# Where a streaming attention step turns its cached keys: TensorE or VectorE

## The chip, the cores and the metric

The kernel runs on one core of a Trainium2 chip. A core has five engines that run side by side, each with its own queue of instructions: TensorE (PE in the profile, with its weight loads as a row of their own, PEld), VectorE (DVE), ScalarE (ACT), GpSimd (POOL) and SyncE (SP), which here issues most of the transfers. The metric is the device time of one execution in microseconds, as the median of several runs.

## The reference, cut to what matters

One layer takes 512 new frames of one stream (the prompt) and 64 next frames of another (the samples), which has 512 cached frames. Both go through the same weights. The attention part, for each of 8 heads of 128 channels, is a stick-breaking attention:

```
z = jnp.einsum('bqhd,bkhd->bhqk', q, k) / math.sqrt(HEAD_DIM)
mask = (k_pos[None, :] < q_pos[:, None])[None, None]
log_1mb = jnp.where(mask, jax.nn.log_sigmoid(-z), 0.0)
after = lax.cumsum(log_1mb, axis=3, reverse=True) - log_1mb
w = jnp.where(mask, jnp.exp(jax.nn.log_sigmoid(z) + after), 0.0)
return jnp.einsum('bhqk,bkhd->bqhd', w.astype(v.dtype), v)
```

The samples' queries see the 512 cached keys and the 64 new ones. Beside it stands a gated convolution over 1024 channels; the outputs of both are normed, put side by side and multiplied by one output projection, and a SwiGLU feed-forward layer follows:

```
mix = jnp.concatenate([rmsnorm(o_attn, g_attn_out), rmsnorm(o_conv, g_conv_out)], axis=-1)
x = x + mix @ w_out
h2 = rmsnorm(x, g_norm2)
x = x + (jax.nn.silu(h2 @ w_gate) * (h2 @ w_up)) @ w_down
```

All data is fp32.

## The kernel before, in words

Prompt and samples lie side by side, channels on the 128 partitions and 576 frames along the free axis (512 prompt, 64 samples). A large product takes each fp32 operand as two fp32r parts, a high one (`whi`, `qh`, `ph`), cast by ACT, and a low one (`wlo`, `ql`, `pl`), the difference, taken by VectorE; three products of parts make one. That pairing of a cast and a subtraction is the helper `split`, and its two lines (L228, L229) appear under most of the names below.

The stages follow one another: the input projection (to about 570 us of the span), the convolution's half of the output projection (`out_proj(mixed_conv, ...)`, to about 748 us), the attention's half, then the feed-forward layer. The attention itself has no stage of its own. It runs inside the convolution's half of the output projection, woven between that half's products.

How it is woven: TensorE's instructions stay in the order in which the program writes them. `product` issues three matmuls of 128x288 and then ticks a counter (`pipe.tick()`); this is a *step*. Generators are registered with the counter; each `yield n` hands back control until n steps later. `heads()` starts one `attend(h)` every 29 steps (`PERIOD`), and one head's generator lasts longer than that, so the end of a head runs among the start of the next. The instructions of ACT, VectorE, GpSimd and SP are not held to the written order: a scheduler places them when the program is built, by its own estimate of when each will be ready. `tc.issue_after(x)` tells it to place what follows behind instruction x. Once placed, an engine runs its queue in order, and a waiting instruction holds all behind it.

One head, in its steps:

- Scores of the prompt, in three blocks (`scores`, L1176 and L1173), each followed by `softplus`: three ACT steps (L1131 to L1133) and one on VectorE (L1134) that reads `z` and writes `pr`. Block 2 comes first.
- Seven steps after its start the samples' scores, `zs` (L1204): one product of the new keys `kf` and four of the cached keys `kcT`, each fp32 and so of two passes, ten passes in all. Then the next head's `qf` and `kf` are loaded into the same buffers.
- The cached keys arrive in `cK` with frames on the partitions (four blocks of 128 frames by 128 channels). The products need channels on the partitions. `keys_cached` has TensorE turn the four blocks into a PSUM buffer `kc` of the pool `ps_pj` (three buffers, shared with the projection's `pjo` and the head's `po`), and ACT copies it to `kcT` (L1157, L1158). Head h does this for head h + 1, and then loads head h + 2's `cK`.
- Sums along the stick (`trir`, `neg1r`), a mask by VectorE (L1229), the exponential (L1231) and a `split`, for each block.
- The prompt's output `po` (L1283) in three parts, with `sample_weights` in between: the samples' sums, a mask on VectorE (L1223) and one exponential on ACT that writes `ws` (L1225).
- `mixed(po, ...)` scales the output into the high and low parts `mixa` (L1273, L1274); squares follow for the norm.
- Two steps later, the samples' output `os_` (L1298): four products of the cached values `cV` and one of the new ones `vtok`, ten passes, each with a part of `ws`. Then `fetch_v` loads the next head's values into the same buffers.

The samples' output of a head and the samples' scores of the next head fall on the same step, 36 steps after the start of the first and 7 after that of the second.

Of the kernel before, what the change touches and what calls it, by code (L numbers as in the profile page):

```python
# [22 lines left out]
BK = 32  # L23
D = 2048
KD = D // P
NH = 8
# [76 lines left out]
def tile_hybrid_stream_step(  # L103
# [6 lines left out]
    nc = tc.nc  # L110
# [3 lines left out]
    ck, cv = cache_k[0, 0], cache_v[0, 0]  # L114
# [26 lines left out]
    def misc(name):  # L141
        return ps_z.tile([P, 512], F32, tag="misc", name=name, bufs=2)
# [84 lines left out]
    def split(hi, lo, src, lo_eng=None):  # L227
        cast = nc.scalar.copy(out=hi, in_=src)  # L228
        (lo_eng or nc.vector).tensor_tensor(out=lo, in0=src, in1=hi.bitcast(F32), op=ALU.subtract)  # L229
        return cast.ins  # L230
# [6 lines left out]
    ident = const.tile([P, P], F32, name="ident")  # L237
# [395 lines left out]
    with tc.manual_schedule(engines={mybir.EngineType.Activation, mybir.EngineType.DVE, mybir.EngineType.SP}):  # L633
# [60 lines left out]
        for kt in range(KD + LAG):  # L694
# [22 lines left out]
            if kt in (7, 11, 17):  # L717
                j = (kt - 7) // 4
# [300 lines left out]
    cK = bpool.tile([P, 4, P], F32, name="cK")  # L1019
    ws = bpool.tile([P, 320], F32, name="ws")  # L1020
    kcT = bpool.tile([P, TP], F32, name="kcT")
    neg1r, trir = (bpool.tile([P, P], F32R, name=name) for name in ("neg1r", "trir"))
    m01, mneg = (bpool.tile([P, P], F32, name=name) for name in ("m01", "mneg"))
    s01, sneg = (bpool.tile([P, TS], F32, name=name) for name in ("s01", "sneg"))
# [14 lines left out]
        split(kh, kl, kf[:, :TP])  # L1039

    def load_cached_keys(h):
        nc.sync.dma_start(out=cK, in_=ck[:, h, :].rearrange("(i p) d -> p i d", p=P))

    def fetch_v(h):
        first = nc.sync.dma_start(out=vtok[:, 4], in_=v_dram[h][T - P :])
# [36 lines left out]
    for h in range(NH):  # L1082
        t = tpool.tile([P, 2, T], F32R, tag=f"t{h}", name=f"mixa{h}")
# [46 lines left out]
    def softplus(dst, ps, scratch):  # L1130
        nc.scalar.activation(out=scratch, in_=ps, func=AF.Abs)  # L1131
        nc.scalar.activation(out=scratch, in_=scratch, func=AF.Exp, scale=-1.0)
        nc.scalar.activation(out=scratch, in_=scratch, func=AF.Ln, bias=1.0)  # L1133
        nc.vector.scalar_tensor_tensor(out=dst, in0=ps, scalar=0.0, in1=scratch, op0=ALU.max, op1=ALU.add)  # L1134

    kw = dict(start=False, skip_group_check=True)
    bt = {}
# [13 lines left out]
        split(bt["v2"][:, 0], bt["v2"][:, 1], vtok[:, 0:2, :])  # L1151
        split(bt["vh"][2], bt["vl"][2], vtok[:, 2, :])

    def keys_cached(h):
        kc = ps_pj.tile([P, 512], F32, tag="pj", name="kc")
        for i in range(4):
            nc.tensor.transpose(kc[:, i * P : (i + 1) * P], cK[:, i, :], ident)  # L1157
        nc.scalar.copy(out=kcT, in_=kc)  # L1158
        if h + 1 < NH:
            load_cached_keys(h + 1)  # L1160

    width = (512, 384, 256)
    full = (512, 384, 384)
# [1 line left out]
    def attend(h):  # L1165
        pr, ph, pl, s1h, s1l, sp = (bt[n] for n in ("pr", "ph", "pl", "s1h", "s1l", "sp"))
        pb = [pr[0], pr[1], pr[2][:, :256], pr[2][:, 256:]]
        z, zb = {}, {}

        def scores(i):  # L1170
            kk, q0 = slice(i * P, (i + 1) * P), i * P
            if i == 3:
                mm(zb[i], kf[:, kk], qf[:, q0:TP], stop=False, **kw)  # L1173
                return
            for n, (a_, b_) in enumerate(((kh, qh), (kh, ql), (kl, qh))):
                mm(zb[i], a_[:, kk], b_[:, q0:TP], start=(n == 0), stop=False, skip_group_check=True)  # L1176

        for b in (2, 1, 0):
            z[b] = ps_z.tile([P, 512], F32, tag=f"z{b}", name=f"z{b}")
            zb[b] = z[b][:, : width[b]]  # L1180
            if b == 2:
                zb[3] = z[b][:, 256:384]
            blocks = (2, 3) if b == 2 else (b,)
            w = full[b]
            for i in blocks:
                scores(i)
            softplus(pr[b][:, :w], z[b][:, :w], pr[b][:, :w])
            for i in blocks:
                nc.gpsimd.tensor_tensor(out=pb[i][:, :P], in0=pb[i][:, :P], in1=m01, op=ALU.mult)  # L1189
            split(ph[b], pl[b], pr[b][:, : width[b]])  # L1190
            if b == 2:
                nc.gpsimd.tensor_tensor(out=pb[2][:, P:], in0=pb[2][:, P:], in1=pb[3], op=ALU.add)
                split(s1h, s1l, pb[2])
            if b == 1:
                nc.gpsimd.tensor_tensor(out=pb[1][:, P:], in0=pb[1][:, P:], in1=pb[2], op=ALU.add)
                split(s0h, s0l, pb[1])
            yield 3 if b else 1
            if h == 0 and b == 1:
                keys_cached(0)

        zs = misc("zs")
        for n, b in enumerate((4, 3, 2, 1, 0)):
# [15 lines left out]
        def sample_weights():  # L1218
            mm(zs[:, :320], trir, sph[:, :320], stop=False, **kw)
            mm(zs[:, :320], trir, spl[:, :320], stop=False, **kw)  # L1220
            mm(zs[:, :256], neg1r, sph[:, 320:], stop=False, **kw)
            mm(zs[:, :256], neg1r, spl[:, 320:], stop=True, **kw)
            nc.vector.scalar_tensor_tensor(out=zs[:, 256:320], in0=zs[:, 256:320], scalar=0.0, in1=sneg,  # L1223
                                           op0=ALU.min, op1=ALU.add)
            nc.scalar.activation(out=ws, in_=zs[:, :320], func=AF.Exp)  # L1225
# [12 lines left out]
        mm(zb[3], trif, pb[3], stop=False, **kw)  # L1238
        mm(zb[2][:, P:], neg1f, pb[3], stop=False, **kw)
# [2 lines left out]
        behind = weights(2)  # L1242
# [8 lines left out]
        behind = weights(1)  # L1251
# [27 lines left out]
        po = ps_pj.tile([P, 512], F32, tag="pj", name="po")  # L1279
        mm(po[:, 384:512], vtok[:, 3, :], pb[3], start=True, stop=False, skip_group_check=True)  # L1280
        for i in (2, 1, 0):
            for n, (a_, b_) in enumerate(((vh, ph), (vl, ph), (vh, pl))):
                mm(po[:, i * P : 512], a_[i], b_[i][:, : 512 - i * P], stop=(i == 0 and n == 2), **kw)  # L1283
# [12 lines left out]
        for b in range(5):  # L1296
            lv = vtok[:, 4, :] if b == 4 else cV[:, b, :]
# [442 lines left out]
```

## Time and profile before

| | us |
|---|---|
| median of 3 runs | 2326.66 (2326.58 to 2326.91) |
| the profiled execution | 2327.18 |
| its span, first to last instruction | 2325.5 |
| TensorE busy | 2315.3 |
| TensorE's weight loads busy | 2306.9 |
| VectorE busy | 1951.5 |
| ScalarE busy | 1222.1 |
| GpSimd busy | 304.3 |

The granted TensorE clock is full over the whole span. The difference between the execution's own time and its span, 1.7 us, lies around the first and the last instruction. Matmuls are pipelined, so two in a row overlap in the records: the distance between two starts, and not the duration of one, tells what an instruction takes from TensorE's time.

### The profile page before, as it was taken

Reading aid. Unit: us, or ns where it says so; the run is one execution under the profiler, and the core shown is the slowest. Engines: PE = TensorE matmul, PEld = TensorE weight load, DVE = VectorE, ACT = ScalarE, POOL = GpSimd, SP = SyncE. Lnnn points to the kernel's source line nnn. Section 1 sums busy time; section 2 is a strip of 40 time slices with the busy share of each in tenths; the row PEclk is TensorE's granted clock in tenths of the full one; section 3 lists DMA queues with packets and bytes.
Section 4 is the critical chain, followed back from the end, with each engine's and each line's share of the span. In section 5 each row is a group of like instructions: output and inputs, shape, how many; then the busy total and the mean of one; then the engine's idle time right before and its main releaser. Section 6 shows DMA issues by size and latency. Waiting matters only on the chain.

```text
span 2325.5 us, 43556 instructions
## 1 busy us (share of the span) xinstructions
PE 2315.3 (100%) x17432; PEld 2306.9 (99%) x17432; DVE 1951.5 (84%) x2871; ACT 1222.1 (53%) x2170; POOL 304.3 (13%) x374
## 2 busy tenths in 40 slices
PE   9999999999999999999999999999999999999999
PEld 9999999999999999999999999999999999999999
DVE  8898989897777898888888888888888777987897
ACT  8566656456887564444444444444444444444443
POOL 0212121110432320000000000000000002431222
PEclk9999999999999999999999999999999999999999
DMA  8444343546653554544444444344344936885654
GB/s 273 136 118 130 91 142 107 147 129 209 191 148 101 173 200 128 155 138 141 149 135 150 131 148 155 112 157 157 117 155 134 351 129 205 228 240 184 209 128 108
DMA packets 533674, 368.57 MB, mean 158 GB/s; under 512 B 70246, under 2 KB 517888, under 8 KB 533472
## 3 DMA queue, kind: packets, MB, share of 16 engines
q1 hardware_dynamic: 526976, 356.42, 48.8%
q0 software_dynamic: 6384, 9.24, 2.3%
q8 instruction: 136, 2.23, 0.4%
q14 instruction: 66, 0.54, 0.1%
q10 hardware_dynamic: 112, 0.14, 0.0%
HBM read 285.52 MB, written 80.23 MB: 157 GB/s over the span
## 4 chain that ended last, share of the span: by engine, by line
PE 94%; ACT 3%; DVE 2%; POOL 1%; issue 0%; DMA 0%; SPq 0%; POOLq 0%; ACTq 0%; DVEq 0%
PE psy L405 47%; PE psw L405 24%; PE psx L405 12%; PE pjo L224 6%; PE pj L691 1%; PE pjz L691 1%; PE psv L405 1%; PE pjm L691 1%; ACT ph L228 0%; PE psx L556 0%; DVE pr L1134 0%; DVE wlo L177 0%; POOL pr L1189 0%; ACT whi L176 0%; DMA vtok<-v_dram 0%
## 5 line engine op out<-in xcount | busy, mean ns | idle before, releaser
L229 DVE TENSOR_TENSOR whl<-raw_a,whl 128x1024 fp32r<-128x1024 f32 (+4 forms) x384 | 429.8, 1120 | 55.5 <-ACT whl L228 54.1
L405 PE MATMUL psy<-t,whl 128*128 128x288 f32 x3000 | 447.0, 294 | 0.0
L228 ACT CAST whl<-raw_a 128x1024 fp32r<-128x1024 f32 (+4 forms) x384 | 360.1, 940 | 140.0 <-PE psx L405 44.9
L405 PE MATMUL psy<-h_s,whl 128*128 128x288 f32 x2766 | 416.6, 294 | 0.0
L405 PEld LDWEIGHTS psy<-t,whl 128*128 128x128 f32 x3000 | 414.4, 188 | 0.0
L405 PE MATMUL psw<-t,whl 128*128 128x288 f32 x2688 | 388.9, 294 | 0.0
L405 PEld LDWEIGHTS psy<-h_s,whl 128*128 128x128 f32 x2766 | 383.1, 188 | 0.2
L405 PEld LDWEIGHTS psw<-t,whl 128*128 128x128 f32 x2688 | 366.8, 188 | 0.0
L228 ACT CAST whl<-raw_b 128x1024 fp32r<-128x1024 f32 (+5 forms) x234 | 211.4, 905 | 208.2 <-issue 71.4
L229 DVE TENSOR_TENSOR whl<-raw_b,whl 128x1024 fp32r<-128x1024 f32 (+5 forms) x234 | 256.1, 1095 | 73.4 <-ACT whl L228 72.4
L428 ACT COPY part<-psy 128x288 f32<-128x288 f32 x309 | 123.2, 399 | 347.9 <-PE psy L405 345.5
L405 PE MATMUL psx<-h_s,whl 128*128 128x288 f32 x1164 | 170.2, 294 | 0.0
L228 ACT CAST whl<-s 128x1024 fp32r<-128x1024 f32 (+5 forms) x103 | 95.3, 925 | 124.3 <-PE psw L405 116.4
L405 PEld LDWEIGHTS psx<-h_s,whl 128*128 128x128 f32 x1164 | 159.6, 188 | 0.0
L405 PE MATMUL psw<-t34a,whl 128*128 128x288 f32 x1056 | 150.4, 295 | 0.0
L405 PE MATMUL psy<-t12a,whl 128*128 128x288 f32 x1056 | 150.4, 295 | 0.0
L405 PEld LDWEIGHTS psw<-t34a,whl 128*128 128x128 f32 x1056 | 143.5, 188 | 0.0
L405 PEld LDWEIGHTS psy<-t12a,whl 128*128 128x128 f32 x1056 | 143.3, 188 | 0.2
L1455 POOL DMA_DIRECT2D hid_dram<-form x7 | 5.2, 736 | 951.6 <-DVE form L229 944.5
L229 DVE TENSOR_TENSOR whl<-s,whl 128x1024 fp32r<-128x1024 f32 (+5 forms) x103 | 110.3, 1071 | 20.3 <-ACT whl L228 19.6
L224 PE MATMUL pjo<-mixc,whi 128*128 128x288 f32 x512 | 118.7, 299 | 0.0
L224 PE MATMUL pjo<-mixa,whi 128*128 128x288 f32 x512 | 102.8, 295 | 0.0
(565 smaller groups left out, 3922.0 us busy)
## 6 DMA issues: line engine op xcount, KB each, us to landing
hid_dram<-form SPq DMA_DIRECT2D x147, 288.0 KB
raw_a<-in_w_in_dram SPq DMA_DIRECT2D x22, 1024.0 KB
raw_b<-in_w_in_dram SPq DMA_DIRECT2D x22, 1024.0 KB
raw_b<-in_w_gate_dram SPq DMA_DIRECT2D x22, 1024.0 KB
raw_b<-in_w_up_dram SPq DMA_DIRECT2D x22, 1024.0 KB
raw_a<-in_w_gate_dram SPq DMA_DIRECT2D x22, 1024.0 KB
raw_a<-in_w_up_dram SPq DMA_DIRECT2D x22, 1024.0 KB
h_s<-hid_dram SPq DMA_DIRECT2D x10, 2016.0 KB
```

Source lines behind the costliest of these rows:

```text
L224: mm(ps, w_[:, k, csl], x_[:, a:b], start=(k == 0 and n == 0), stop=(k == nk - 1 and n == 2))
L228: cast = nc.scalar.copy(out=hi, in_=src)
L229: (lo_eng or nc.vector).tensor_tensor(out=lo, in0=src, in1=hi.bitcast(F32), op=ALU.subtract)
L405: mm(ps, whl[:, w_, j, :], x_, start=(start and j == 0 and q == 0), stop=(j == len(xs_) - 1 and q == 2), skip_group_check=True)
L428: nc.scalar.copy(out=t, in_=st["y"])
L691: mm(banks_[c][i], w3[:, kt % 8, c * P : (c + 1) * P], t[:, x_, :], start=(kt == 0 and n == 0), stop=(kt == KD - 1 and n == 2))
L1455: q.dma_start(out=hid_dram[fp][2 * n - 2 : 2 * n].rearrange("f p t -> p f t"), in_=t.bitcast(F32))
```

## The change

The cached keys of head 0 are loaded and turned as before. For heads 1 to 7 the load is in four pieces, each of 32 channels: piece g writes partitions g to g + 31, and on partition j of it stand, for every 32nd frame from j on, 32 channels in a row (runs of 128 bytes). So each block of 32x32 holds what the turned keys need there, only turned within the block, and one stream transpose by VectorE from `cK` to `kcT`, which turns each 32x32 block by itself, does the rest. It is placed behind the head's own softplus of block 2, instead of a step of the head before. The four TensorE transposes, the buffer `kc` and ACT's copy remain in head 0 only.

The samples' output comes three steps after `mixed`, not two. And `mixed(po, ...)` has to be placed behind the samples' mask and exponential.

```diff
@@ load_cached_keys
-        nc.sync.dma_start(out=cK, in_=ck[:, h, :].rearrange("(i p) d -> p i d", p=P))
+        if h == 0:
+            nc.sync.dma_start(out=cK.rearrange("p (i d) -> p i d", d=P), in_=ck[:, h, :].rearrange("(i p) d -> p i d", p=P))
+            return
+        for g in range(0, P, BK):
+            nc.sync.dma_start(out=cK[g : g + BK].rearrange("j (t d) -> j t d", d=BK),
+                              in_=ck[:, h, g : g + BK].rearrange("(t j) d -> j t d", j=BK))
@@ keys_cached, now first_keys
-    def keys_cached(h):
+    def first_keys():
         kc = ps_pj.tile([P, 512], F32, tag="pj", name="kc")
         for i in range(4):
-            nc.tensor.transpose(kc[:, i * P : (i + 1) * P], cK[:, i, :], ident)
+            nc.tensor.transpose(kc[:, i * P : (i + 1) * P], cK[:, i * P : (i + 1) * P], ident)
         nc.scalar.copy(out=kcT, in_=kc)
-        if h + 1 < NH:
-            load_cached_keys(h + 1)
@@ attend
-            softplus(pr[b][:, :w], z[b][:, :w], pr[b][:, :w])
+            behind = softplus(pr[b][:, :w], z[b][:, :w], pr[b][:, :w])
+            if h and b == 2:
+                with tc.issue_after(behind):
+                    nc.vector.transpose(out=kcT, in_=cK)
...
         if h + 1 < NH:
-            keys_cached(h + 1)
+            load_cached_keys(h + 1)
...
-                sample_weights()
+                mask, exp = sample_weights()
                 yield 2
-        mixed(po, 0, TP)
+        with tc.issue_after(mask), tc.issue_after(exp):
+            mixed(po, 0, TP)
         nc.scalar.activation(out=sq[0], in_=po[:, :HALF], func=AF.Square)
         squares(0)
         nc.scalar.activation(out=sq[1][:, : TP - HALF], in_=po[:, HALF:], func=AF.Square)
-        yield 2
+        yield 3
```

How the queues of the built programs differ, at three places (lines of the changed program carry its own numbers). On TensorE, at the step that head 0's output and head 1's scores share, before and then with the change; `pjo` is the projection's product:

```order
L224 MATMUL pjo<-mixc,whi_6605 128x288
L1298 MATMUL zs<-ws,cV 128x64 x4
L1298 MATMUL zs<-ws,vtok 128x64
L1204 MATMUL zs<-qf,kf 128x64
L1204 MATMUL zs<-qf,kcT 128x64 x4
L224 MATMUL pjo<-mixc,whi_6605 128x288
L224 MATMUL pjo<-mixc,wlo_6606 128x288
```

```order
L224 MATMUL pjo<-mixc,whi_6605 128x288
L1210 MATMUL zs<-qf,kf 128x64
L1210 MATMUL zs<-qf,kcT 128x64 x4
L224 MATMUL pjo<-mixc,whi_6605 128x288
L224 MATMUL pjo<-mixc,wlo_6606 128x288
L224 MATMUL pjo<-mixc,whi_6605 128x288
L1305 MATMUL zs<-ws,cV 128x64 x4
L1305 MATMUL zs<-ws,vtok 128x64
```

The scores now stand ahead, and the output behind them and one step of three products; it is so in heads 1 to 7.

On VectorE, at the softplus of block 2 of head 6, with the split of a projection weight (`wlo`) ahead of it:

```order
L177 TENSOR_TENSOR wlo_8233<-raw_a,whi_8232 128x512 x3
L229 TENSOR_TENSOR pl_6703<-pr_6700,ph_6702 128x512
L177 TENSOR_TENSOR wlo_8233<-raw_a,whi_8232 128x512
L1134 SCALAR_TENSOR_TENSOR pr_6701<-z_8251,pr_6701 128x384
L1223 SCALAR_TENSOR_TENSOR zs<-zs,sneg 128x64
L229 TENSOR_TENSOR hbe<-pr_6701,hbe 128x256
```

```order
L177 TENSOR_TENSOR wlo_8219<-raw_a,whi_8218 128x512 x3
L229 TENSOR_TENSOR pl_6703<-pr_6700,ph_6702 128x512
L1139 SCALAR_TENSOR_TENSOR pr_6701<-z_8237,pr_6701 128x384
L1193 STREAM_TRANSPOSE kcT<-cK 128x512
L1229 SCALAR_TENSOR_TENSOR zs<-zs,sneg 128x64
L1115 TENSOR_TENSOR pjo<-pjo,accc 128x288
```

The transpose stands between the softplus and the samples' mask of the head before, in all seven heads; one of the four splits moved away ahead of this piece.

On ACT, at the same place; `ph` is the high part of head 5's block 0, and the L1131 of `z_8251` the first softplus step of head 6:

```order
L1231 ACTIVATE pr_6700<-z_8075 128x512
L176 CAST whi_8232<-raw_a 128x512
L228 CAST ph_6702<-pr_6700 128x512
L1131 ACTIVATE pr_6701<-z_8251 128x384
L1132 ACTIVATE pr_6701<-pr_6701 128x384
```

```order
L1237 ACTIVATE pr_6700<-z_8064 128x512
L1136 ACTIVATE pr_6701<-z_8237 128x384
L228 CAST ph_6702<-pr_6700 128x512
L1137 ACTIVATE pr_6701<-pr_6701 128x384
L1138 ACTIVATE pr_6701<-pr_6701 128x384
```

The two have changed places, and the cast of a weight is gone from between. On ACT the exponential of `ws` stands ahead of `mixa<-po` in both programs. On SP the pieces of a head's cached keys are issued partly ahead of the next head's `qf` and `kf` and partly behind its values; the loads of `vtok` and `cV`, which stood ahead of `qf` and `kf`, now stand behind them.

More of the change, by code (lines that the diff above doesn't have):

```diff
@@ L1018, in tile_hybrid_stream_step @@
     qh, ql, kh, kl = (bpool.tile([P, TP], F32R, name=name) for name in ("qh", "ql", "kh", "kl"))
-    cK = bpool.tile([P, 4, P], F32, name="cK")
+    cK = bpool.tile([P, TP], F32, name="cK")
     ws = bpool.tile([P, 320], F32, name="ws")
@@ L1133, in softplus @@
         nc.scalar.activation(out=scratch, in_=scratch, func=AF.Ln, bias=1.0)
-        nc.vector.scalar_tensor_tensor(out=dst, in0=ps, scalar=0.0, in1=scratch, op0=ALU.max, op1=ALU.add)
+        return nc.vector.scalar_tensor_tensor(out=dst, in0=ps, scalar=0.0, in1=scratch, op0=ALU.max, op1=ALU.add).ins
     kw = dict(start=False, skip_group_check=True)
@@ L1198, in attend @@
             if h == 0 and b == 1:
-                keys_cached(0)
+                first_keys()
         zs = misc("zs")
@@ L1222, in sample_weights @@
             mm(zs[:, :256], neg1r, spl[:, 320:], stop=True, **kw)
-            nc.vector.scalar_tensor_tensor(out=zs[:, 256:320], in0=zs[:, 256:320], scalar=0.0, in1=sneg,
-                                           op0=ALU.min, op1=ALU.add)
-            nc.scalar.activation(out=ws, in_=zs[:, :320], func=AF.Exp)
+            mask = nc.vector.scalar_tensor_tensor(out=zs[:, 256:320], in0=zs[:, 256:320], scalar=0.0, in1=sneg,
+                                                  op0=ALU.min, op1=ALU.add)
+            return mask.ins, nc.scalar.activation(out=ws, in_=zs[:, :320], func=AF.Exp).ins
         def weights(b):
```

## The prediction, made before the changed kernel ran

> **What bounds the kernel now.** I read the page's busy shares first, then the waits of TensorE over the stretch in which the changed functions run, and then that stretch cut at one repeating mark. From the page:
>
> ```profile
> span 2325.5 us, 43556 instructions
> PE 2315.3 (100%) x17432; PEld 2306.9 (99%) x17432; DVE 1951.5 (84%) x2871; ACT 1222.1 (53%) x2170; POOL 304.3 (13%) x374
> ```
>
> TensorE is busy for 2315.3 of 2325.5 us. So time is saved only by taking work off TensorE or by closing gaps in its queue, and lost only by opening gaps. The heads run from about 574 to 750 us. In the list of waits of TensorE's weight loads from 560 to 780 us, all the gaps are small:
>
> ```profile
> PEld zs L1298 <- ACT ws L1225: 2.2, 5, 0.9
> PEld po L1283 <- DVE pl L229: 0.7, 2, 0.4
> PEld po L1283 <- ACT ph L228: 0.5, 1, 0.5
> PEld zs L1204 <- ACT kcT L1158: 0.4, 1, 0.4
> PEld z L1176 <- DVE kl L229: 0.2, 1, 0.2
> ```
>
> Columns: microseconds in total, times, longest. The largest is the samples' output product, L1298, waiting for the samples' weights `ws`. These are waits of the loads, so what they cost has to be read from the pace. I cut the stretch at the first L1298 of heads 0 to 6; each row is one head's period.
>
> ```profile
> 604.89:625.35 20.46, 20.46 (x154) 20.11 (x153) 14.79 (x32) 17.41 (x40) 7.98 (x15) 1.00 0.55 151
> 625.35:646.72 21.37, 21.28 (x154) 20.14 (x152) 15.40 (x32) 17.18 (x40) 8.62 (x15) 1.00 0.53 146
> 646.72:667.32 20.60, 20.60 (x151) 20.07 (x151) 14.96 (x33) 17.02 (x40) 7.94 (x15) 1.00 0.45 110
> 667.32:689.00 21.68, 21.18 (x152) 20.02 (x151) 16.85 (x37) 17.50 (x40) 6.72 (x14) 1.00 0.36 114
> 689.00:710.30 21.30, 20.67 (x152) 20.09 (x152) 16.00 (x36) 17.12 (x39) 6.47 (x14) 1.00 0.39 122
> 710.30:731.20 20.90, 20.72 (x151) 20.13 (x151) 16.84 (x37) 17.14 (x40) 6.86 (x13) 1.00 0.29 96
> ```
>
> Columns: the stretch, its length, then busy time of PE, PEld, DVE, ACT and POOL, granted clock (full), share of the DMA engines, GB/s. The same tensor work is done in each, so the first, 20.46, is a head without a gap, and the others are longer by 0.91, 0.14, 1.22, 0.84 and 0.44: 3.55 us in all is lost to waits. ACT (17 of 20.5) and DVE (15 to 17) are the engines that are waited for.
>
> **The turning taken off TensorE: a gain of 3.05 us.** One group of four transposes, from TensorE's timeline:
>
> ```profile
> 716.09 0.29 PE L224 MATMUL pjo<-mixc,whi 128*128 128x288 f32 x1
> 716.23 0.60 PE L1157 MATMUL kc<-ident,cK 128*128 128x128 f32 x4
> 716.58 0.38 PE L224 MATMUL pjo<-mixc,whi 128*128 128x288 f32 x1
> 716.80 0.29 PE L224 MATMUL pjo<-mixc,wlo 128*128 128x288 f32 x1
> 716.93 0.29 PE L224 MATMUL pjo<-mixc,whi 128*128 128x288 f32 x1
> ```
>
> Durations overlap, so I count starts. The last two starts lie 0.13 apart. From the first `whi` to `wlo` 0.71 us pass where two steps of 0.13 to 0.14 would stand: the group costs 0.44, including the slow first load behind it. Head 0 keeps its group, so 7 x 0.435 = 3.05. [...] With the groups go seven copies of ACT:
>
> ```profile
> L1158 ACT COPY kcT<-kc x8: 566/584/591, 585.2 to 717.8; 128x512 f32<-128x512 f32 x8
> ```
>
> That is 0.58 us less on ACT per head, worth nothing by itself since TensorE is the bound, but it gives room to the engine that is waited for. The PSUM buffer `kc` no longer takes a turn among the three of its pool; no wait for that pool stands above, so nothing is counted.
>
> **The turning put on VectorE: 0.70 us per head, off the path.** A stream transpose on this chip took:
>
> ```profile
> L1608 DVE STREAM_TRANSPOSE ob<-acc_z x2: 465/468/470, 2221.8 to 2227.0; 128x288 f32<-128x288 f32 x2
> L807 DVE STREAM_TRANSPOSE tok<-E-20_1697 x1: 770/770/770, 159.5 to 159.5; 128x576 f32<-128x576 f32 x1
> ```
>
> A column costs (770 - 468) / 288 = 1.05 ns, so 512 columns cost 468 + 224 x 1.05 = 703 ns. It stands right behind the softplus of block 2 (L1134) and ahead of the samples' mask (L1223). Two queues hang on it. First TensorE's sample scores, which read `kcT`. Second, on DVE itself, the mask and all behind it. The tightest head:
>
> ```profile
> 707.96 0.56 DVE L1134 SCALAR_TENSOR_TENSOR pr<-z,pr 128x384 f32<-128x384 f32 x1 [0.21 <-ACT pr L1133]
> 708.43 0.22 DVE L1223 SCALAR_TENSOR_TENSOR zs<-zs,sneg 128x64 f32<-128x64 f32 x1
> ...
> 709.25 0.19 PEld L224 LDWEIGHTS pjo<-mixc,whi 128*128 128x128 f32 x1
> 710.30 0.97 PEld L1298 LDWEIGHTS zs<-ws,cV 128*128 128x128 f32 x8 [0.86 <-ACT ws L1225]
> ```
>
> The transpose would start where the mask does, at 708.43, and end at 709.13. The scores now come first in TensorE's queue, right behind the load at 709.25: 0.14 later, and 0.22 more for the two passes on the new keys, so `kcT` is needed at 709.6. That leaves 0.5 us in the head that waits longest for ACT. So I take nothing lost. Bounds: 0 below, 7 x 0.70 = 4.9 above, if every transpose lay wholly on the path. DVE's load rises to 15.5 to 17.6 of 20, still under ACT's.
>
> **The samples' outputs one step later: a gain of about 2 us.** L1298 moves behind the scores (ten passes) and one step of three products. How long ten passes take:
>
> ```profile
> 747.75 0.29 PE L224 MATMUL pjo<-mixc,whi 128*128 128x288 f32 x1
> ...
> 749.12 0.30 PE L224 MATMUL pjo<-mixa,wlo 128*128 128x288 f32 x1
> ```
>
> Between these lie ten passes and two steps of 0.13: 1.37 - 0.27 = 1.10. So L1298 gets 1.10 + 0.40 = 1.50 us more for `ws`. The longest wait was 0.86 by its row, or 710.30 - 709.25 - 0.14 = 0.91 by starts, and the mask lies at most 0.70 later behind the transpose: 0.91 + 0.70 is 0.1 over the 1.50 in the worst head and under it in all others. I take the whole 2.2 of the list as gone (by starts it is nearer 2.4). Today the twenty passes stand together; in a gapless head, by the same count:
>
> ```profile
> 625.34 0.29 PE L224 MATMUL pjo<-mixc,whi 128*128 128x288 f32 x1
> ...
> 627.84 0.29 PE L224 MATMUL pjo<-mixc,wlo 128*128 128x288 f32 x1
> ```
>
> 2.50 - 0.27 = 2.23 against twice 1.10: parting them costs nothing.
>
> Of the other gaps (`pl`, `ph`, `kl`, 1.3 us together), ACT's and DVE's new order takes some and gives some: the masks of `z` and ACT's exponentials of block 1 come earlier, but block 0's cast `ph` now stands behind the next head's first softplus step, 0.5 us later. One row of DVE against one of TensorE shows what is left at the tightest place:
>
> ```profile
> 706.46 0.69 DVE L229 TENSOR_TENSOR pl<-pr,ph 128x512 fp32r<-128x512 f32 x1
> ...
> 707.56 0.19 PEld L1283 LDWEIGHTS po<-pl,hbe 128*128 128x128 f32 x1
> ```
>
> 707.15 against 707.56: 0.4 of slack, so about 0.1 of new wait there. Given and taken, I count nothing; bounds are a gain of 1.3 and a loss of 0.7, if each of seven heads had only this slack.
>
> **The mixed output queued behind the exponential: nothing.** ACT's order already has `ws` ahead of `mixa<-po` in every head. The new wait only pins it. Behind the waiting `mixa` stand ACT's casts of the next head, and no row of `mixa<-po` is waited for.
>
> **The new loads: nothing.** One load per head becomes four, of 128-byte runs. SP's queue took 0.4 us to issue one load of the old kind:
>
> ```profile
> 686.83 0.38 SPq L184 DMA_DIRECT2D raw_a<-in_w_out_dram  x1
> ...
> 695.54 0.38 SPq L1042 DMA_DIRECT2D cK<-in_cache_k_dram  x1
> 707.83 0.38 SPq L184 DMA_DIRECT2D raw_a<-in_w_out_dram  x1
> ```
>
> SP stood idle for 12 us between the last two, so three more issues of about 0.4 find room. The price on the DMA engines, from a stretch in which only 128-byte runs were stored:
>
> ```profile
> 2230.00:2235.00 5.00, 5.00 (x40) 5.00 (x39) 4.84 (x6) 2.22 (x4) 1.69 (x2) 1.00 0.27 43
> ```
>
> A share of 0.27 for 43 GB/s means 159 GB/s at full share, so 256 KB cost 1.6 us of a 20 us period in which the share is 0.29 to 0.55. The later pieces of a head are issued behind the values' loads, about 15 us ahead of its transpose. Two pieces of head 6, which wait for head 5's transpose, now stand ahead of the weight load that went out at 686.83; it goes out some 5 us later, behind the values, and its slot is read only in the next weight's turn, 20 us on. With that cover gone the transpose would wait and all of DVE behind it. Bounds: 0, and for each us that a landing is late, that us once per head less the slack of 0.5.
>
> **The sum.** Profiled execution 2327.18 us (its span 2325.5 and 1.7 around it). Less 3.05, less 2.2, the other terms zero: 2321.9. That execution lies 0.5 above the median of 2326.66, so for the median 2321.4, 0.23% less.
>
> **Rivals.** *The gaps stay.* Periods of 21 us could be ACT's own pace: 17 busy and in-order waits around it. Then TensorE, 0.44 sooner per head, only waits elsewhere. For it speak the rows of 21.68 and 21.30, where `ph` and `pl` waits join those for `ws`; against it the 20.46 with the same 17.4 on ACT, and that ACT loses 0.58 per head. It gives 2326.66 - 3.05 = 2323.6, and with 0.2 of new waits per head 2325.0.
>
> *VectorE becomes the bound.* The transpose finds DVE late, so sample scores wait for `kcT` in seven heads. Slower by over 0.2% (4.65 us) needs 4.65 + 5.25 = 9.9 us of waits, 1.4 per head: behind a slack of 0.5 or more that means a `kcT` some 2 us late, three DVE instructions of 0.7. For it: three splits of a weight (`wlo`) stand just ahead of that softplus in the tightest head. Against it: there DVE still had an idle 0.21 before L1134. It decides where TensorE's wait for `kcT` exceeds 0.75 per head; at 1.5 per head the time is 2332. [...]
>
> *All gaps close.* ACT's 0.58 of room and the earlier masks also end the waits for `pl`, `ph` and `kl`: 2326.66 - 3.05 - 3.55 = 2320.1. The rows of 20.46 and 20.60 show that gapless heads exist; that `ph` comes 0.5 later speaks against it.
>
> *The queueing does nothing.* The third part's wait pins what is so already, as said; its time is that of the forecast.
>
> **Numbers.** Forecast (a gain of 4 to 6): 0.52. All gaps close: 0.12. Gaps stay: 0.26. VectorE late: 0.10, of which 0.07 beyond +0.2%. The bound of 0.2% is about what a measurement of this kernel can tell from no change. The forecast lies just beyond it, so 0.09 of its own chance counts as same: faster 0.43 + 0.12 = 0.55, same 0.09 + 0.26 + 0.03 = 0.38, slower 0.07. The range goes from 2319.9 (all gaps closed, and 0.2 of head 0's) to 2325.2 (gaps stay, 0.2 per head of new waits); what it leaves out is the late VectorE and a little on each side.
>
> **What would show it.** Right: no L1157 from head 1 on; seven stream transposes of about 0.70 us; no wait of L1298 for `ws`; periods near 20.0. Wrong: TensorE waiting for `kcT` or for `pl` and `ph` in several heads (gaps moved), DVE waiting for a load of `cK` (cover gone), or periods still at 21.

## The result, and the profile after

The changed kernel takes 2322.43 us (median of 16 runs, 2321.55 to 2323.51); the kernel before, run beside it, 2327.81 (16 runs, 2326.58 to 2329.01). The ratio is 0.9977, with a 95% interval from 0.997 to 0.9984: faster by 5.4 us, between 3.7 and 7.0. The profiled execution took 2323.28. From its page:

```profile
span 2321.6 us, 43509 instructions
PE 2310.5 (100%) x17404; PEld 2303.5 (99%) x17404; DVE 1952.7 (84%) x2878; ACT 1216.2 (52%) x2163; POOL 303.7 (13%) x374
```

28 TensorE transposes fewer, 7 VectorE instructions more, 7 ScalarE instructions fewer. The lines of the changed program have other numbers: the samples' scores stand at L1210, their output at L1305, the exponential that writes `ws` at L1231. The waits of TensorE's weight loads, 560 to 780 us, as before (us in total, times, longest):

```profile
PEld zs L1210 <- ACT kcT L1163: 1.0, 1, 1.0
PEld z L1179 <- DVE kl L229: 0.8, 2, 0.4
PEld po L1289 <- DVE pl L229: 0.6, 1, 0.6
PEld po L1289 <- DVE hbe L229: 0.4, 1, 0.4
PEld z L1179 <- ACT kh L228: 0.2, 1, 0.2
```

In this list no product waits for `ws` any more, and none in heads 1 to 7 for turned keys; the wait for `kcT` is head 0's, which TensorE still turns. The new instruction, by its line:

```profile
L1193 DVE STREAM_TRANSPOSE kcT<-cK x7: 700/702/702, 604.4 to 726.5; 128x512 f32<-128x512 f32 x7
```

The stretch cut at the first sample output of heads 0 to 6, as before (length, busy PE, PEld, DVE, ACT, POOL, granted clock, DMA share, GB/s):

```profile
607.69:627.69 20.00, 20.00 (x150) 19.64 (x149) 15.20 (x34) 16.54 (x38) 7.76 (x14) 1.00 0.76 188
627.69:648.56 20.87, 20.52 (x150) 19.76 (x149) 15.58 (x33) 16.63 (x39) 8.23 (x15) 1.00 0.58 145
648.56:668.54 19.98, 19.98 (x150) 19.63 (x148) 16.12 (x35) 16.51 (x39) 8.32 (x14) 1.00 0.66 159
668.54:688.49 19.95, 19.95 (x149) 19.60 (x148) 16.83 (x37) 16.41 (x38) 7.00 (x13) 1.00 0.28 74
688.49:708.85 20.36, 20.22 (x150) 19.52 (x149) 16.80 (x37) 16.31 (x39) 6.49 (x14) 1.00 0.51 154
708.85:728.86 20.01, 20.01 (x150) 19.66 (x149) 16.34 (x36) 15.94 (x37) 5.95 (x12) 1.00 0.33 88
```

A head without a gap now takes 20.0 us, not 20.46. The six periods add up to 121.17 against 126.31: 5.14 less, of which 6 x 0.46 = 2.8 is a gapless head's gain and the remaining 2.4 are gaps that closed. Two gaps are left: 0.87 in the second row (waits for `hbe` and `kl`) and 0.36 in the fifth (for `pl`).

The two spans differ by 3.9 only, less than the medians, because this execution reached the first mark late: its heads 1 to 7 start some 1.3 us later than the step's shift of 1.5 explains, with the 1.0 for `kcT` among it. Two later runs, in which every engine's queue stands in the same order (the two paces, below), show no such wait, and runs of nearly the same program reached that mark between 605.9 and 607.1 us. That is the spread of single executions, and one profiled execution should not be read against another to the last microsecond.

### The profile page after: what moved, and what is told of

It is laid out like the page before. It is cut to its first block, busy times and chain, and to the rows that moved or that the text cites. A ratio compares the mean times of both kernels' runs of the same rounds, so it can differ in the third digit from the quotient of the medians.

```text
span 2321.6 us, 43509 instructions
## 1 busy us (share of the span) xinstructions
PE 2310.5 (100%) x17404; PEld 2303.5 (99%) x17404; DVE 1952.7 (84%) x2878; ACT 1216.2 (52%) x2163; POOL 303.7 (13%) x374
## 4 chain that ended last, share of the span: by engine, by line
PE 94%; DVE 2%; ACT 2%; POOL 1%; DMA 1%; issue 0%; SPq 0%; POOLq 0%; ACTq 0%; DVEq 0%
PE psy L405 47%; PE psw L405 24%; PE psx L405 12%; PE pjo L224 5%; PE pj L691 1%; PE pjz L691 1%; PE psv L405 1%; PE pjm L691 1%; DVE wlo L177 0%; DVE pl L229 0%; PE psx L556 0%; DMA vtok<-v_dram 0%; ACT ph L228 0%; ACT pr L1237 0%; DVE z L1235 0%
```

## The experiments

All were run in rounds beside the kernel before, on one chip in each group of four. Gains are differences of medians against it.

### One part at a time

The turning alone, with the samples' output two steps behind `mixed` as before, and no queueing:

```diff
         mask, exp = sample_weights()
...
-        with tc.issue_after(mask), tc.issue_after(exp):
-            mixed(po, 0, TP)
+        mixed(po, 0, TP)
...
-        yield 3
+        yield 2
```

> The turning alone: heads 1 to 7 turned by VectorE, the samples' output two steps after the mixed output as before, no queueing. By the theory of the prediction (0.435 us per head taken off TensorE, the waits for ws closed by the later step alone): 3.05 us less than before, less what the mask, now up to 0.70 us later behind the transpose, adds to the waits for ws, so a gain of 0 to 3 us, and waits of L1305 for ws of 2.2 us or more in the list. By the rival that the gaps are ScalarE's pace and close because it loses the copies: a gain of 4 to 5 us with few waits for ws left.

Measured: 2328.67 against 2327.59, ratio 1.0004 (0.9995 to 1.0013). The turning alone gains nothing, less than the 0 to 3 us that were expected. Its waits, and three of its periods:

```profile
PEld zs L1304 <- ACT ws L1231: 3.2, 4, 2.4
...
665.93:689.10 23.17, 20.48 (x148) 19.59 (x148) 18.90 (x41) 18.44 (x43) 7.43 (x15) 1.00 0.51 148
689.10:710.70 21.60, 21.60 (x148) 21.26 (x148) 15.64 (x35) 16.27 (x37) 6.67 (x13) 0.92 0.35 94
710.70:730.71 20.01, 20.01 (x149) 19.66 (x148) 16.52 (x36) 16.05 (x38) 5.74 (x12) 1.00 0.34 95
```

A gapless head does take 20.01, so TensorE's time is freed; it is lost again in the waits for `ws`, 2.38 of it in one head. The row after that wait is odd: 21.60 with no wait in it and a granted clock of 0.92. That comes back in the last section. In all, the six periods of this execution take 126.67, where the kernel before took 126.31: the group gives 2.8 (6 x 0.46), but the gaps grew from 3.55 to 5.1, and the lowered clock took 1.6.

The later output alone, on the kernel before (TensorE turns as before):

```diff
-        yield 2
+        yield 3
```

> The kernel before with the samples' output one step later and nothing else: all eight heads turned by TensorE. By the theory: the waits for ws go, a gain of 2.2 to 2.4 us, periods of 20.5 us where no other gap is. By the rival that the gaps are ScalarE's pace: within 0.5 us of before, and periods of 21 us stay, the waits having moved to pl and ph.

Measured: 2325.06, ratio 0.999 (0.9981 to 0.9999), a gain of 2.5. All waits for `ws` are gone:

```profile
PEld po L1283 <- DVE pl L229: 0.7, 2, 0.4
PEld pjo L224 <- DVE x L1111: 0.2, 1, 0.2
...
606.66:627.11 20.45, 20.45 (x153) 20.10 (x152) 15.43 (x33) 17.87 (x41) 8.23 (x14) 1.00 0.58 153
627.11:647.52 20.41, 20.41 (x153) 20.04 (x152) 14.46 (x31) 16.45 (x38) 7.96 (x14) 1.00 0.57 151
```

So the step is worth 2.5 alone, and with the step in place the turning is worth what is left of the 5.4, about 2.9 by the medians; the gapless periods, 20.45 here and 20.0 in the changed kernel, say the same. Without the step it is worth nothing. The parts don't add up: TensorE's half microsecond per head is usable only where it does not wait for `ws`.

Was it the step, or the queueing, that the turning alone lacked? The changed kernel with two steps but with the queueing:

```diff
-        yield 3
+        yield 2
```

> The changed kernel with its samples' outputs put back two steps behind the mixed output: VectorE's turning and the queueing of the mixed output stay. The run with the turning alone gained nothing and waited 3.2 us for the samples' weights. Theory A: what is missing there is the step; the step alone takes those waits away, and without it the waits stay whatever the order of the mixed output is. Gain against the kernel before 0 to 2 us, waits of the samples' output product for the weights 2 to 4 us in all. Theory B: what was missing there is the queueing (in one head the mixed output's scaling stood ahead of the exponential, and that head waited 2.4 us); with it the longest wait is under 1 us, the waits for the weights are under 1.5 us in all, and the gain is 3 to 4 us.

Measured: 2326.77 against 2327.47, ratio 0.9998 (0.9989 to 1.0007).

```profile
PEld zs L1305 <- ACT ws L1231: 2.6, 4, 1.8
...
667.23:689.81 22.58, 20.53 (x148) 19.61 (x148) 17.94 (x39) 17.34 (x41) 7.44 (x15) 1.00 0.49 144
689.81:711.39 21.58, 21.58 (x148) 21.23 (x149) 16.68 (x37) 16.88 (x39) 6.49 (x13) 0.92 0.38 100
```

Theory A holds: with the queueing, the waits for `ws` stay, 2.6 for 3.2. In the turning alone one head had the scaling ahead of the exponential; the queueing mends that, and by the medians it buys 1.8 us there, with intervals that overlap. Not all of that is the order: in six of these eleven executions the mean granted clock was 1.000, in the turning alone in two of eleven. Those six took 2325.35 to 2326.77, those two 2326.56 and 2327.24, so about 1 us is left for the order. In the whole change the queueing buys nothing: built with the later step and without the queueing, every engine's queue comes out the same, instruction for instruction. That is read from the built programs, not from a run.

### What VectorE's turning costs

The changed kernel without its seven transposes. The cached keys of heads 1 to 7 are left out of the result.

```diff
-            if h and b == 2:
-                with tc.issue_after(behind):
-                    nc.vector.transpose(out=kcT, in_=cK)
```

> The changed kernel without its seven stream transposes: heads 1 to 7 use the turned keys of head 0, so the cached keys of those heads are left out of the result; their loads stay. Theory: VectorE's 0.70 us per head lies beside TensorE's work, so the time is that of the changed kernel within 1 us (a gain of 4.5 to 6.5 against the kernel before). Rival: VectorE's queue is what leaves the remaining gaps of heads 2 and 5 open; then these close too, and the gain is 6.5 to 8 us, with six periods all within 20.0 to 20.1.

Measured: 2322.69, ratio 0.9979 (0.997 to 0.9988). Within 0.3 of the changed kernel by the medians, 0.6 by the gains: the seven instructions of 0.70, which would add 4.9 if they lay on the path, cost nothing that can be seen. The gaps did not close for want of them either; they moved (periods of 20.00, 20.22, 20.45, 20.39, 20.55 and 20.01), so the rival falls.

Each of the seven done twice:

```diff
                 with tc.issue_after(behind):
-                    nc.vector.transpose(out=kcT, in_=cK)
+                    for _ in range(2):
+                        nc.vector.transpose(out=kcT, in_=cK)
```

> The changed kernel with each of the seven VectorE transposes done twice in a row, 0.70 us more per head on VectorE at that place. It measures the slack that the prediction put at 0.5 us in the tightest head. By the theory: TensorE waits for kcT in some heads for 0.2 us or less, 0 to 1.4 us more than the changed kernel. By the rival that VectorE is close to being the bound: 0.70 in every head, 4.9 us more, which takes the gain away.

Measured: 2322.41, ratio 0.9978 (0.9969 to 0.9987). By the median, nothing again. But the profiled execution, with 2323.66 the second slowest of eleven, is not that of the changed kernel:

```profile
PEld zs L1306 <- ACT ws L1232: 1.2, 1, 1.2
...
666.06:687.14 21.08, 20.11 (x149) 19.53 (x147) 17.65 (x40) 16.87 (x40) 6.53 (x13) 1.00 0.42 118
687.14:708.76 21.62, 21.62 (x148) 21.28 (x149) 17.50 (x39) 17.58 (x41) 6.59 (x13) 0.92 0.41 117
```

One head did run out of slack: a wait of 1.2 for `ws` at the end of the first row shown, not for `kcT` as was expected, and again a long row with a lowered clock behind it. The wait is longer than the 0.7 added, so the order of the queues had a part in it. The gaps of the changed kernel were closed in exchange: less the 1.6 of the lowered clock, the six periods add up to 121.1, as in the changed kernel (121.17). The lowered clock is not in the median: eight of the eleven executions, the median one among them, had a mean granted clock of 1.000. So five heads of the six had room for 0.7 us more on VectorE, and the tightest had not.

### What TensorE's turning cost

The later output alone, on the kernel before, with TensorE's transposes of heads 1 to 7 doubled:

```diff
-        for i in range(4):
+        for i in [i for i in range(4) for _ in range(2 if h else 1)]:
             nc.tensor.transpose(kc[:, i * P : (i + 1) * P], cK[:, i, :], ident)
```

> The kernel before with the samples' outputs one step later alone, as in an earlier run (gain 2.5 us, no wait for the samples' weights), and with each of TensorE's four transposes of heads 1 to 7 done twice. Without those waits a price on TensorE cannot hide. Theory: a group of four costs 0.44 us of TensorE's time, so this is 3.05 us slower than without the doubling: 0 to 1.5 us slower than the kernel before, periods near 20.9. [...]

Measured: 2327.57 against 2327.43, ratio 0.9999 (0.999 to 1.0007), 2.7 slower than without the doubling by gains against the kernel before. The periods are the clean answer:

```profile
606.53:627.41 20.88, 20.88 (x157) 20.52 (x156) 15.25 (x33) 17.37 (x41) 8.26 (x14) 1.00 0.56 149
627.41:648.25 20.84, 20.84 (x157) 20.49 (x156) 14.85 (x32) 16.68 (x38) 8.03 (x14) 1.00 0.56 149
...
710.75:731.64 20.89, 20.89 (x157) 20.54 (x156) 17.55 (x37) 17.65 (x42) 7.04 (x13) 1.00 0.28 84
```

Gapless periods of 20.00 with no group, 20.45 with one and 20.88 with two: 0.44 us for each group of four.

### The loads

Every piece loaded twice into the same tile:

```diff
-        for g in range(0, P, BK):
+        for g in [g for g in range(0, P, BK) for _ in range(2)]:
```

> The changed kernel with every piece of the cached keys of heads 1 to 7 loaded twice, eight loads per head and 512 KB. Theory: the loads are covered by about 15 us; the time is that of the changed kernel within 1 us, and VectorE's transposes wait for no load. The weight's load behind the waiting pieces goes out later and is still not waited for. Rival: SP's queue or the DMA engines are near their limit; then the transposes or the casts of the next weight wait for a load, and the gain against the kernel before falls under 3 us.

Measured: 2353.87, ratio 1.0109 (1.0095 to 1.0122). Much slower, but not for the reason that the rival names. The scheduler placed the transposes later in VectorE's queue; that it did so because it has each second load wait for the first to land was the author's estimate, and no row here shows it. The first transpose, on VectorE and then on TensorE:

```profile
606.44 0.55 DVE L229 TENSOR_TENSOR pl<-hbl,ph 128x384 fp32r<-128x384 f32 x1
606.90 0.71 DVE L1193 STREAM_TRANSPOSE kcT<-cK 128x512 f32<-128x512 f32 x1
```

```profile
604.23 0.32 PEld L1210 LDWEIGHTS zs<-qf,kf 128*128 128x128 f32 x2
607.67 1.78 PEld L1210 LDWEIGHTS zs<-qf,kcT 128*128 128x128 f32 x8 [3.11 <-DVE kcT L1193]
```

VectorE waited for nothing ahead of it; the transpose stood behind the split of block 1 (`pl`) and others that in the changed kernel come after it, and TensorE waited 3.11. In all heads together TensorE waited 17.1 us for `kcT`, and the run is 31 us slower than the changed kernel. In the profiled execution most of what goes beyond the waits goes with the granted clock, which was 0.50 in three stretches of 6.8, 10.2 and 10.2 us, each beginning in or right behind a wait of over 3 us (last section). So this run says nothing of the loads' cover. It shows the rival in which VectorE turns too late, and its price.

The same load beside, into a tile that nobody reads, 48 KB a piece:

```diff
             nc.sync.dma_start(out=cK[g : g + BK].rearrange("j (t d) -> j t d", d=BK),
                               in_=ck[:, h, g : g + BK].rearrange("(t j) d -> j t d", j=BK))
+            nc.sync.dma_start(out=cK2[g : g + BK].rearrange("j (t d) -> j t d", d=BK),
+                              in_=ck[:384, h, g : g + BK].rearrange("(t j) d -> j t d", j=BK))
```

> The changed kernel with a second load behind each piece of the cached keys of heads 1 to 7, of 48 KB of the same rows in the same 128-byte runs, into a tile that nobody reads: 448 KB per head in eight loads in place of 256 KB in four. Unlike the earlier doubling into the same tile, no load waits for the one before it; the program is otherwise the same but for the place of some weight splits and masks in the queues of VectorE and ScalarE. Theory: the loads are covered; no stream transpose waits for a load, the transposes stand in their places, and the gain against the kernel before is 4 to 6.5 us, as without them. Rival: the loads are near the limit of SyncE's queue or of the DMA engines; then a transpose or a cast of the next head's operands waits for a load by more than 0.5 us, and the gain falls under 3 us.

Measured: 2321.73 against 2327.43, ratio 0.9976 (0.9966 to 0.9986): no slower than the changed kernel, so the loads are covered, with 448 KB per head as with 256. The periods:

```profile
605.93:625.93 20.00, 20.00 (x149) 19.64 (x148) 16.01 (x34) 16.92 (x40) 7.53 (x14) 1.00 0.59 121
625.93:645.91 19.98, 19.98 (x149) 19.63 (x148) 14.86 (x33) 16.13 (x37) 8.08 (x14) 1.00 0.74 192
...
706.13:726.31 20.18, 20.18 (x149) 19.73 (x148) 16.54 (x36) 15.88 (x38) 6.03 (x13) 1.00 0.48 129
```

Six heads take 120.38, within 0.4 of six gapless ones. Besides the loads, what differs is the order of some instructions of VectorE, ScalarE and GpSimd, weight splits (`wlo`, L177) among them. At the place of the remaining wait for `pl` (head 5), VectorE in the changed kernel, and then here:

```profile
700.79 0.68 DVE L177 TENSOR_TENSOR wlo<-raw_a,whi 128x512 fp32r<-128x512 f32 x1
...
703.09 1.88 DVE L177 TENSOR_TENSOR wlo<-raw_a,whi 128x512 fp32r<-128x512 f32 x3
704.90 0.68 DVE L229 TENSOR_TENSOR pl<-pr,ph 128x512 fp32r<-128x512 f32 x1
```

```profile
699.70 1.88 DVE L177 TENSOR_TENSOR wlo<-raw_a,whi 128x512 fp32r<-128x512 f32 x3
701.53 0.69 DVE L229 TENSOR_TENSOR pl<-pr,ph 128x512 fp32r<-128x512 f32 x1
702.14 0.69 DVE L177 TENSOR_TENSOR wlo<-raw_a,whi 128x512 fp32r<-128x512 f32 x1
```

There all four pieces of a weight's split stand ahead of `pl`; here three do, as in the kernel before, and the fourth stands behind it. From start to start a piece takes 0.6, about what TensorE waits for `pl` in the changed kernel (0.58). That makes it the likely cause of that gap; other instructions moved too, so it is not shown. The medians of the two kernels differ by 0.7 and their intervals overlap, so this is no better kernel shown.

### Two tries at the last gaps

The pieces of a weight's split every eight steps, and every six, in place of seven:

```diff
                 weight_parts(raws[j][:, :2048], hi, lo, a, a + 512, nc.vector)
-                yield 7
+                yield 8
```

> The changed kernel with the pieces of a projection weight's split every eight steps in place of seven. Theory: the gaps left in heads 2 and 5 (waits of 0.4 to 0.6 for hbe, kl and pl) come from weight splits that stand ahead of the waited-for instruction on VectorE; with another pace they go from there or stand in other heads, and the sum of the six periods moves by up to 1.5 us either way: a gain of 4 to 7 us against the kernel before. Rival: the gaps are set by the head's own chain over GpSimd and ScalarE; then the same heads keep the same gaps, and the time is that of the changed kernel within 0.5 us.

> The changed kernel with those pieces every six steps. The same two theories as for eight: gaps in other heads and a sum of periods up to 1.5 us off, or the same gaps in heads 2 and 5. A gain of 4 to 7 us against the kernel before.

Measured: 2322.54 (ratio 0.998, 0.9971 to 0.9989) and 2322.77 (0.9979, 0.997 to 0.9988). The waits for `pl`, `kl` and `hbe` stand where they stood in the changed kernel. That is the rival's outcome, but it decides nothing, because the edit moved nothing: in both traces every engine runs the changed kernel's instructions in the changed kernel's order, from the first to the last, and in the built programs only numbers of buffers differ. So these two runs cannot tell theory and rival apart. They are the changed kernel measured twice more, and its 2322.43 came back as 2322.54 and 2322.77. For the cause of the gaps, the rows of the loads beside are the only evidence, and no run moved those splits alone.

### Head 0 by VectorE too

```diff
-            if h and b == 2:
+            if b == 2:
                 with tc.issue_after(behind):
                     nc.vector.transpose(out=kcT, in_=cK)
...
-            if h == 0 and b == 1:
-                first_keys()
```

> The changed kernel with head 0's cached keys loaded in pieces and turned by VectorE as well, so that no transpose of keys and no copy is left on TensorE and ScalarE. By the theory: 0.44 us less than the changed kernel for the group, and up to 1.0 us for TensorE's wait for the copy in head 0, so 5.8 to 6.8 us less than before. Against it: the transfers are at their busiest when head 0 starts (0.95 to 0.99 of the engines), so 2048 short runs could land after the softplus and hold VectorE; then the first head starts later and the gain shrinks by that wait.

Measured: 2325.16, ratio 0.9991 (0.9982 to 1.0): a gain of 2.4, where 6 was expected. GpSimd's queue had been built with the sums of head 0's samples ahead of the adding of block 2 to block 1 (L1192). GpSimd, and the cast on ScalarE that waits for it:

```profile
595.10 1.04 POOL L1207 TENSOR_TENSOR hbl<-hbl 128x64 f32<-128x64 f32 x2
596.10 0.74 POOL L1192 TENSOR_TENSOR hbl<-hbl,pr 128x256 f32<-128x256 f32 x1
```

```profile
596.87 0.51 ACT L228 CAST s0h<-hbl 128x384 fp32r<-128x384 f32 x1 [2.75 <-POOL hbl L1192]
```

With that adding pinned ahead of the samples' sums in every head:

```diff
-                nc.gpsimd.tensor_tensor(out=pb[1][:, P:], in0=pb[1][:, P:], in1=pb[2], op=ALU.add)
+                sums_1 = nc.gpsimd.tensor_tensor(out=pb[1][:, P:], in0=pb[1][:, P:], in1=pb[2], op=ALU.add).ins
...
-        nc.gpsimd.tensor_tensor(out=sp[:, 256:320], in0=sp[:, 256:320], in1=s01, op=ALU.mult)
+        with tc.issue_after(sums_1):
+            nc.gpsimd.tensor_tensor(out=sp[:, 256:320], in0=sp[:, 256:320], in1=s01, op=ALU.mult)
```

> All eight heads turned by VectorE, as in the earlier run, and each head's sums of the samples on GpSimd placed behind its adding of block 2 to block 1. In the earlier run head 0's adding stood behind the samples' sums in GpSimd's queue, so that the cast s0h and TensorE behind it waited (0.9 and 0.4 us). Theory: this order is what cost the earlier run its gain; now the waits for s0h and s0l are gone and the gain against the kernel before is 4.5 to 7 us, 2 to 4 more than in the earlier run. Rival: head 0's loads and its start in the crowded DMA stretch cost it; then the gain stays at 2 to 3.5 us.

Measured: 2323.63, ratio 0.9983 (0.9974 to 0.9992), a gain of 3.8. The waits for `s0h` and `s0l` are gone and 1.4 us came back, so the order was part of the cause; but the gain lies between the 4.5 that the theory gave and the 3.5 of its rival, and still 1.2 to 1.5 under the changed kernel's, with intervals that overlap. Waits for `kcT`, `pl` and `ph` of 1.0 in all stand in head 0. The transpose of head 0 waits for no load there: it starts at 585.00, right behind the split of `hbe`, which had waited 1.1 for ScalarE. By the medians, turning head 0 on TensorE stays the better choice; how much of the rest is due to the crowded start (a DMA share of 1.06 to 1.13 from 574 to 582 us in the changed kernel), and how much to the order, was not settled.

## Why the prediction was right

It gave 2321.4 us with a range of 2319.9 to 2325.2 and faster at 0.55; measured were 2322.43, and 5.4 us of gain against its 5.25. The gain is the fair comparison: the kernel before took 1.15 more beside the changed one than in the three runs from which the forecast starts.

- *The turning taken off TensorE, 3.05.* The price of a group, read from a distance of starts, was 0.44; periods of 20.00, 20.45 and 20.88 give 0.44. Right, but only together with the later step: alone it gained nothing. The prediction added the terms; that the first rests on the second stands only in its rival of the gaps that stay.
- *The turning on VectorE, nothing.* A transpose takes 702 ns where 703 were worked out. Taking all seven away changes nothing that can be seen. The head for which a slack of 0.5 was worked out has 0.85 (turned at 706.71, read at 707.57), but it is not the tightest: head 7, which the prediction did not look at, has 0.34 (727.24 and 727.58).
- *The samples' output a step later, 2.2.* 2.5 alone, and no wait for `ws` is left in the changed kernel. Right. The head that was reckoned 0.1 over has 1.2 to spare (`ws` written at 707.62, read at 708.85); the least of all is 0.5.
- *The other gaps, nothing given or taken.* The gaps of six heads fell from 3.55 us to 1.17 (121.17 less six times 20.0), which is the 2.2 to 2.4 of the `ws` waits: the sum of the others stayed near 1.2. The zero held, but it was in part luck: they are other gaps in other places, and other orders of the queues left 0.4 (the loads beside) or 1.6 (without VectorE's transposes). In the tightest place 0.1 of new wait was expected and 0.58 came (the wait for `pl`): this is the term that was mis-sized. From a slack of 0.4 the prediction took only the 0.5 by which the cast `ph` comes later, and that is not what `pl` waited for: `ph` ended at 704.53, and `pl` started at 704.90, right behind the splits. Not counted were the 0.44 by which TensorE comes sooner in each head, and the fourth piece of the weight's split, 0.6, that now stands ahead of `pl`. 0.4 of slack less these two makes a wait of 0.6, close to the 0.58; that is worked out from the traces, and neither was tried alone.
- *The queueing, nothing.* With the later step, the queues are the same with and without it. Without the step it does change the order in one head.
- *The loads, nothing.* Right with 1.75 times the bytes; the weight's load behind them goes out late, at 692.41 where it went out at 686.83, and nobody waits for it. SyncE held on the pieces for 15.7 us in the profile, until the transpose of the head before was done (at 686.17), and then had nothing overdue behind it:

```profile
671.32 15.73 SPq L1046 DMA_DIRECT2D cK<-in_cache_k_dram  x4
688.39 0.35 SPq L1034 DMA_DIRECT2D qf<-qk_dram  x1
```

Of the rivals, *the gaps stay* is what happens without the later step (1.1 us slower and 0.7 us faster by the medians, where it gave a gain of 3.05: the waits for `ws` grew, and the clock of the last section came on top). *VectorE becomes the bound* happened in the run in which its transposes stood too late, and cost more than the waits themselves (31 us by the medians, 17.1 of waits in the profile). *All gaps close* is nearly what the run with loads beside shows, at 2321.73.

## What to carry to other kernels

Work taken off the engine that is the bound was gained here only where that engine did not then wait for the next thing sooner (0.44 us a head: nothing alone, about 2.9 in all with the later step): move the waiting product back in the same change, and measure both alone and together. Read an instruction's price from the distance of starts and from whole periods, not from its duration (a group of four transposes was 0.60 long in the records and took 0.44). Where a scheduler sets the queues, a small edit can shift the time by a microsecond (1.4 came back with the place of one adding in GpSimd's queue), or move nothing at all, as the change of pace did. Compare the queues before crediting the edit, and pin the order that matters.

## What the runs showed of the hardware

In some profiled executions a wait of TensorE cost more than its length. In the profiled execution with VectorE's transposes doubled, TensorE waited 1.2 us up to 687.14; the granted clock in slices of about 1 us around it:

```profile
686.00:687.20 1.20, 0.23 (x3) 0.06 (x1) 0.73 (x2) 1.20 (x4) 0.00 (x0) 1.00 1.12 361
687.20:688.20 1.00, 1.00 (x10) 1.00 (x10) 0.64 (x2) 1.00 (x3) 0.72 (x1) 1.00 1.12 356
688.20:689.20 1.00, 1.00 (x8) 1.00 (x8) 0.25 (x1) 1.00 (x4) 0.12 (x1) 0.66 0.69 267
689.20:690.20 1.00, 1.00 (x6) 1.00 (x6) 0.29 (x1) 1.00 (x5) 0.68 (x1) 0.50 0.31 89
...
691.20:692.20 1.00, 1.00 (x7) 1.00 (x6) 1.00 (x3) 0.00 (x0) 0.33 (x1) 0.63 1.03 289
692.20:693.20 1.00, 1.00 (x10) 1.00 (x9) 0.37 (x2) 0.84 (x3) 0.47 (x3) 1.00 1.12 172
```

Some 1.4 us after the wait the clock falls to half for 3.4 us, with TensorE busy throughout, and that period is 21.62 long where 20.0 would be due: 1.6 us lost beside the 1.2 waited. The same stands 2.6 us behind the wait of 2.38 in the turning alone (21.60) and 2.3 us behind that of 1.8 in the run with two steps (21.58). Waits of 1.01 (head 0 of the changed kernel) and 0.9 (the kernel before) were followed by no such fall.

But the length of a wait alone did not decide it. In the run with every piece loaded twice, two waits of 1.9 were followed by 20 us at full clock, first the waits and then the stretches behind them:

```profile
652.78 0.97 PEld L1210 LDWEIGHTS zs<-qf,kcT 128*128 128x128 f32 x8 [1.90 <-DVE kcT L1193]
703.48 0.97 PEld L1210 LDWEIGHTS zs<-qf,kcT 128*128 128x128 f32 x8 [1.94 <-DVE kcT L1193]
```

```profile
652.79:672.90 20.11, 20.11 (x147) 19.67 (x147) 13.83 (x30) 14.75 (x35) 6.77 (x14) 1.00 0.65 145
703.49:723.60 20.11, 20.11 (x147) 19.66 (x147) 14.30 (x33) 14.36 (x34) 5.05 (x13) 1.00 0.44 109
```

Nor did the program. A fall of 3.4 us to half takes 0.0007 off the mean granted clock of an execution (1.7 of some 2325 us); with the doubled transposes eight of eleven executions had a mean of 1.000, with two steps six of eleven, and in the turning alone two. Going by these averages, the same program runs with such a fall and without it. Whether its waits were as long in the executions without is not on record, and what decides was not found. The fall, 1.6 us in each profile, is part of why the two runs without the later step lost more than their waits. It was no term of the prediction, which counted a microsecond waited as a microsecond lost; in the profiled execution of the changed kernel, without such waits in heads 1 to 7, the granted clock was 1.00 in every row.
